# Program order set from a build-time account of engine times, with the delta rule's preparation, its scan and the convolutions as separate parts

## The chip, the cores and the metric

The kernel runs on one core of a Trainium2 chip. The metric is the device time of one execution in microseconds (us). The core's engines are named as in the profile: PE is the matmul engine (TensorE), DVE is VectorE, ACT is ScalarE, POOL is GpSimd, SP is SyncE, which here only issues DMA transfers. Each engine executes its own queue of instructions in the order in which the program placed them, and waits at an instruction until its operands are there.

## What is computed

One layer of a hybrid model on 640 tokens: 128 context tokens and 512 latent tokens, 2048 columns wide. The tokens are normalised and modulated, projected by `w_in`, and then go through two kinds of mixing: four Fourier groups (a two-dimensional FFT, real part) and twelve heads of a bidirectional gated delta rule. The results, each multiplied by its SiLU gate, go through one output projection, a gated residual and a final norm.

```python
h = rms_norm(x) * (1 + scale) + shift
u_f, z_f, qkv, z_d, ab = split(h @ w_in)
y_f = fourier_mix(u_f) * silu(z_f)
q, k, v = silu(short_conv(qkv))            # three taps along the tokens
q, k = l2norm(q) / sqrt(128), l2norm(k)
# per head and direction, S is 128 x 128; g, beta from ab
S_t = g_t (I - beta_t k_t k_t^T) S_{t-1} + beta_t k_t v_t^T
o_t = S_t^T q_t
# in chunks: A = I + strict_lower(beta k k^T decay);  T = A^-1
# u = T (beta v); w = T (beta k e^g); v_new = u - w S; S = S e^gl + kd^T v_new
y_d = rms_norm(o_forward + o_backward) * silu(z_d)
out = final_norm(x + gate * (concat(y_f, y_d) @ w_out)),  state_new = S at the end of the context
```

## The kernel before, in words

The 640 tokens are five tiles of 128; tile 0 is the context. Up to about 185 us the kernel computes the norm, the modulation and the columns of the first head. Then `stream()` (L1003) runs over 50 tiles of 128 columns of `w_in`. For each tile it issues 96 matmuls of 128x320 at L1015: 16 row blocks, three passes of a high and low part each, two halves of the tokens. The weights are loaded by ACT's DMA queue and split by ACT (L136) and POOL (L137). From head 2 on a head is four such tiles, k, v, q and the gate z of the head before, 384 stream matmuls. Behind the stream `out_stream()` multiplies 16 blocks of y by `w_out`, 15 matmuls of 128x512 to a block in its first pass (L1208). The blocks come in the order heads 0 to 10, Fourier groups 0 to 3, head 11.

Beside the stream run Python generators, which issue the small work between the stream's matmuls:

- **Convolution**: `conv` (L538) works on the finished tile of k, v or q at once, on ACT and DVE (L548 to L554).
- **Solve** of head h, `solve(h)` (L596): the inverse of the chunk's triangular matrix. PE's matmuls pk (L624), then DVE's masks, a trip through memory that lays the blocks out as NP (L643, L646), on DVE small steps of growing size (L658 multiply, L660 sum), and then ten product pairs (`prod`: L670 multiply, L672 sum), 512 or 1024 wide on 40 partitions. It ends in DD (L689 to L695), loaded from memory again.
- **Delta** of head h, `delta(h)` (L701), one generator for both of these. *Preparation*: v to tokens (L563), the gate matrices E and the products with q and k (L722 to L728), then a chain of PE groups with copies between them: px (L740), YT (L753), ET (L768, which needs TA from DVE, L756 and L757), EU (L775), the norm of q as jq (L786) and q (L790, a small DVE instruction on PE's result). *Scan*: five steps, in each of which both directions advance one tile. PE: pks and pqs (L805, L812) from the state S; DVE: r (L808); PE: pv (L823); ACT: vn (L826); PE: pu and po (L831, L844); DVE: S (L839). The first step needs neither S nor r; the last has no pu.
- **Head out** (L870), **Fourier** group f (L899; matmuls L928, L935, L940), **residual gates** (L959).

The order is set by hand-written numbers. Each `yield lat, busy` of a generator says how long its step takes and how much of PE's time it adds. A clock advances by 0.82 with each piece of six stream matmuls and by 3.25 with each 15 matmuls of the output projection. A generator is resumed once the clock has passed its due time. The stream itself waits in one place: a k or q tile of head h may be consumed only when `delta(h-2)` is issued, a v tile when v of head h-1 has been read (`needs`, L1086). A scheduler of the framework then orders among instructions that are ready; what it makes of both programs is what the rows of the built order below show.

## Time and profile before

| what | before |
|---|---|
| time of three runs | 1528.46, 1534.41, 1538.11 us (median 1534.41) |
| the profiled execution: time, span | 1528.22 us, 1526.2 us |
| PE busy | 1407.7 us, 92% |
| weight loads on PE (beside the matmuls) | 1270.9 us, 83% |
| DVE busy | 882.6 us, 58% |
| ACT busy, POOL busy | 635.1 us, 643.5 us, 42% each |

The span is the time between the first and the last record of the profiled execution; about 2 us lie around it. A busy share is an average over the whole span. An engine's idle time counts only where the end of the kernel waits for it, so the views below go by stretches and by waits.

### The profile page before, as it was taken

How to read it: one execution, taken by the hardware profiler on the slowest of the kernel's cores; microseconds unless marked ns; L12 is line 12 of the kernel's file. 1: busy time of each engine (PE TensorE's matmuls, PEld its weight loads, DVE VectorE, ACT ScalarE, POOL GpSimd, SP SyncE). 2: the span in 40 equal slices, each digit the busy share in tenths (PEclk: the TensorE clock that was granted, in tenths of full speed). 3: DMA queues.
4: the chain of work that ended last, by engine and by line, in shares of the span. 5: the costliest groups of instructions: out<-in, count | busy, mean ns of one | idle time of the engine just before them, and what ended most of it. 6: DMA issues, size and time to landing. Idle time of an engine off the chain costs nothing. (4 is left out here: it accounts for less than half of the span.)

```text
span 1526.2 us, 27377 instructions
## 1 busy us (share of the span) xinstructions
PE 1407.7 (92%) x10548; PEld 1270.9 (83%) x10548; DVE 882.6 (58%) x1594; ACT 635.1 (42%) x1678; POOL 643.5 (42%) x759
## 2 busy tenths in 40 slices
PE   6999989889989998989999898999999999999996
PEld 5676989788878897978999898888988998888885
DVE  4455257586867677394756748394856534422025
ACT  5343375244262543526254353526353244322234
POOL 2223346425252542434364344444363433236575
PEclk9999999899999999999999999999999999999999
DMA  9899434315253544433223223323233336386103
GB/s 309 294 336 318 149 114 124 86 39 148 89 157 104 153 119 121 136 96 84 76 84 82 77 80 89 91 72 85 77 95 96 104 114 193 120 301 193 56 1 138
DMA packets 251664, 198.35 MB, mean 130 GB/s; under 512 B 43465, under 2 KB 221590, under 8 KB 251406
## 3 DMA queue, kind: packets, MB, share of 16 engines
q1 hardware_dynamic: 130926, 124.77, 25.5%
q10 hardware_dynamic: 120608, 71.84, 16.5%
q8 instruction: 83, 1.36, 0.4%
q14 instruction: 47, 0.39, 0.1%
HBM read 172.57 MB, written 23.99 MB: 129 GB/s over the span
## 5 line engine op out<-in xcount | busy, mean ns | idle before, releaser
L137 POOL TENSOR_TENSOR wlo<-raw,whi 128x512 fp32r<-128x512 f32 (+1 forms) x276 | 382.1, 1389 | 583.1 <-ACT whi L136 481.1
L1015 PE MATMUL mbank<-h_hi,whi 128*128 128x320 f32 x1600 | 522.9, 327 | 0.0
L1015 PE MATMUL mbank<-h_hi,wlo 128*128 128x320 f32 x1600 | 506.9, 317 | 4.3 <-POOL wlo L137 4.2
L1015 PE MATMUL mbank<-h_lo,whi 128*128 128x320 f32 x1600 | 506.8, 317 | 0.0
L1015 PEld LDWEIGHTS mbank<-h_hi,whi 128*128 128x128 f32 x1600 | 309.8, 194 | 10.5 <-issue 7.9
L1015 PEld LDWEIGHTS mbank<-h_hi,wlo 128*128 128x128 f32 x1600 | 308.6, 193 | 7.3 <-POOL wlo L137 5.6
L1015 PEld LDWEIGHTS mbank<-h_lo,whi 128*128 128x128 f32 x1600 | 309.8, 194 | 1.9 <-issue 1.6
L136 ACT CAST whi<-raw 128x512 fp32r<-128x512 f32 (+1 forms) x276 | 168.2, 614 | 241.1 <-PE mbank L1015 60.8
L670 DVE TENSOR_TENSOR tmp<-NP,XB 40x1024 f32<-40x1024 f32 (+1 forms) x60 | 109.9, 1832 | 1.3
L670 DVE TENSOR_TENSOR tmp<-XB,YB 40x1024 f32<-40x1024 f32 (+1 forms) x60 | 105.8, 1763 | 1.0
L818 POOL TENSOR_SCALAR kd<-k,edl 128x128 f32<-128x128 f32 x96 | 59.8, 634 | 41.6 <-PE bank L831 41.4
L548 ACT COPY pj<-mbank 128x128 f32<-128x128 f32 (+2 forms) x99 | 30.0, 339 | 87.5 <-PE mbank L1015 68.1
L1208 PE MATMUL mbank<-wlo,y_hi 128*128 128x512 f32 x160 | 62.8, 393 | 2.8 <-POOL wlo L137 2.0
L805 PE MATMUL bank<-S,KT 128*128 128x128 f32 x192 | 36.5, 301 | 30.4 <-DVE S L839 30.4
L1208 PE MATMUL mbank<-whi,y_hi 128*128 128x512 f32 x160 | 63.8, 399 | 0.0
L726 ACT ACTIVATE E<-gb,ngg 128x128 f32<-128x128 f32 x120 | 42.2, 394 | 51.8 <-DVE AT L728 31.6
L1208 PE MATMUL mbank<-whi,y_lo 128*128 128x512 f32 x160 | 62.4, 390 | 0.0
L1208 PE MATMUL bank<-whi,y_lo 128*128 128x512 f32 x160 | 62.3, 389 | 0.0
L1208 PE MATMUL bank<-whi,y_hi 128*128 128x512 f32 x160 | 62.3, 389 | 0.0
L1208 PE MATMUL bank<-wlo,y_hi 128*128 128x512 f32 x160 | 62.2, 389 | 0.0
L672 DVE TENSOR_REDUCE YB<-tmp 40x64 f32<-40x512 f32 (+2 forms) x60 | 59.7, 995 | 1.4
L672 DVE TENSOR_REDUCE XB<-tmp 40x64 f32<-40x512 f32 (+2 forms) x60 | 59.7, 995 | 1.3
(319 smaller groups left out, 2440.8 us busy)
## 6 DMA issues: line engine op xcount, KB each, us to landing
raw<-in_w_in ACTq DMA_DIRECT2D x104, 512.0 KB
wm<-in_w_mod SPq DMA_DIRECT2D x64, 512.0 KB
gw<-in_w_mod SPq DMA_DIRECT2D x32, 512.0 KB
raw<-in_w_out ACTq DMA_DIRECT2D x48, 256.0 KB
gb<-gd SPq DMA_DIRECT2D x12, 640.0 KB
yd<-zs SPq DMA_DIRECT2D x16, 320.0 KB
zl<-yd SPq DMA_DIRECT2D x16, 320.0 KB
yd<-zl SPq DMA_DIRECT2D x16, 320.0 KB
```

Of the source, the lines that this page charges most:

```text
L136: ACT.copy(whi, raw_part)
L137: sub.tensor_tensor(wlo, raw_part, whi, ALU.subtract)
L548: ACT.copy(pj[:, a:b], ps)
L670: DVE.tensor_tensor(tv, A.unsqueeze(2).broadcast_to(s4), B.rearrange("p j c -> p c j").unsqueeze(1).broadcast_to(s4), ALU.mult)
L672: DVE.tensor_reduce(dst, tv, AX.X, ALU.add)
L726: ACT.activation(E[:, 1 - d], gb[:, d, P * t:P * (t + 1)], AF.Exp, bias=ngg4[:, d, h, t:t + 1])
L805: PE.matmul(pks[:, P * d:P * (d + 1)], lhsT=KT[:, a:a + P], rhs=S[:, d], start=True, stop=True)
L818: POOL.tensor_scalar(kd[:, d], k[:, tt[d], :], edl4[:, d, h, tt[d]:tt[d] + 1], 1.0, ALU.mult, ALU.mult)
L1015: PE.matmul(pm[:, 0:320], lhsT=w, rhs=h[k][:, a:b], start=n == 0, stop=n == 3 * NK - 1)
L1208: PE.matmul(acc[t], lhsT=a[kk][:, sl], rhs=w, start=kk == order[0] and j == 0, stop=kk == order[-1] and j == 2)
```

## The change

It replaces the hand-written numbers by an account. A class `Estimate` is called at every instruction that the program issues. It keeps, for each engine, when it would be free, and for each tile when it would be written and read; the cost of an instruction comes from a small formula per engine. A generator's step now yields nothing. It is resumed when the estimated end of what it issued last, plus 0.2, has been reached by PE's estimated time, or it says "poll" and is asked again.

Further: `delta` becomes two generators, `prep` (up to q) and `scan`, so that the preparation of the next head may stand ahead of the scan of this one. The convolutions and the gate tiles become generators in steps; a k, v, q, z or f tile counts as done at the end of these, not at their start. The Fourier groups also wait for the delta of head 10. The load of DD waits until the head before has used DD. The tiles v and th get two buffers instead of one. Every engine is issued the same instructions as before.

```diff
+class Estimate:
+    MATMUL, WIDE = 13.5, 1 / 2.4
...
+    def __call__(self, inst, *_):
...
+        t = self.free[engine]
+        for x in ins:
+            y = self.of(x.tensor)
+            t = max(t, y[0] + (0.1 if y[1] != engine else 0.0))
...
+            end = t + self.cost(op, engine, inst, outs, ins)
+            self.free[engine] = end
...
+    est = Estimate()
+    nc.push_inst_callback(est)
...
-    def conv(col, parts, dst):
+    def conv(kind, h, parts):
...
         ACT.mul(dst, pj[:, 0:641], cw[:, ct:ct + 1])
+        yield
         DVE.scalar_tensor_tensor(dst, pj[:, 1:642], cw[:, 36 + ct:37 + ct], dst, ALU.mult, ALU.add)
         DVE.scalar_tensor_tensor(dst, pj[:, 2:643], cw[:, 72 + ct:73 + ct], dst, ALU.mult, ALU.add)
+        yield
+        th = g.tile([P, 641], F32, tag="th", name="th", bufs=2)
         ACT.activation(th, dst, AF.Tanh)
+        yield
         DVE.scalar_tensor_tensor(dst, th, 1.0, dst, ALU.add, ALU.mult)
+        yield
+        done.add((kind, h))
...
         for c0 in (0, 8):
             prod(X2[:, 24:32, c0:c0 + 8], X2[:, 24:32, 16:32], YB[:, :, c0:c0 + 8])
-            yield 3.00, 0
+            yield
         xd = dram.tile([40, 32, 32], F32, tag="xd", name="xd", bufs=2)
         SP.dma_start(out=xd, in_=X2)
+        while h and ("dd", h - 1) not in done:
+            yield "poll"
...
-    def delta(h):
+    def prep(h):
         s = st_h[h]
-        KT, QT, k = s["KT"], s["QT"], s["k"]
-        s["v"] = v = g.tile([P, 5, P], F32, tag="v", name="v", bufs=1)
+        KT, QT = s["KT"], s["QT"]
+        s["v"] = v = g.tile([P, 5, P], F32, tag="v", name="v", bufs=2)
...
         s["q2"] = q2 = g.tile([P, 5], F32, tag="q2", name="q2", bufs=3)
         DVE.tensor_scalar(q2, pq[:, 0:320].rearrange("p (t c) -> p t c", c=64)[:, :, 0], HD * EPS, HD * EPS * EPS, ALU.mult, ALU.add)
+
+
+    def scan(h):
+        s = st_h[h]
+        KT, QT, k, v, T, AT = [s[x] for x in ("KT", "QT", "k", "v", "KK", "AT")]
         while h and ("out", h - 1) not in done:
-            yield 5.50, 0
+            yield "poll"
...
+    def advance():
+        moved = True
+        while moved:
+            moved = False
+            for x in list(live):
+                while x in live and (x[2] is None or x[2] + GUARD <= est.free["PE"]):
+                    poll = x[2] is None
+                    resume(x)
+                    if poll and x[2] is None:
+                        break
+                    moved = True
...
-            while not {("u", f), ("f", f), "E_last"} <= done:
-                yield 8.00, 0
+            while not {("u", f), ("f", f), "E_last", ("delta", NH - 2)} <= done:
+                yield "poll"
...
-    live = [[x(), 0.0] for x in (outs, deltas, solves, fouriers, res_gates)]
-    clock, running = 0.0, True
+    for i, kind in enumerate("kvq"):
+        begin(1, conv(kind, 0, i + 1))
+    for rank, steps in enumerate((outs, scans, preps, solves, fouriers, res_gates)):
+        begin(2 * rank, steps())
+    running = True
```

What this does to the order is counted in the built programs, in stream matmuls of 128x320 on PE:

| head | 3 | 4 | 5 | 6 | 7 | 8 | 9 |
|---|---|---|---|---|---|---|---|
| product pairs on DVE between the first and the last r of the scan, before | 7 | 9 | 8 | 8 | 8 | 8 | 8 |
| the same, after | 2 | 2 | 7 | 3 | 3 | 7 | 3 |
| from the first pv of the scan to its last po, before | 202 | 206 | 200 | 200 | 200 | 200 | 200 |
| the same, after | 55 | 51 | 123 | 85 | 65 | 118 | 81 |
| from pk of the next head to this scan's first pv, before | 132 | 114 | 138 | 138 | 138 | 138 | 138 |
| the same, after | 257 | 270 | 163 | 241 | 259 | 164 | 239 |
| from YT to ET in the preparation, before | 24 | 24 | 24 | 24 | 24 | 24 | 24 |
| the same, after | 54 | 60 | 36 | 24 | 60 | 36 | 24 |

On DVE, before, at the start of a scan in the middle of the stream (XB, YB, NP and tmp are solve's, r and S the scan's, QT the convolution's):

```order
L778 COPY KK<-bank 64x5x64
L790 TENSOR_SCALAR q_8994<-bank 128x5
L551 SCALAR_TENSOR_TENSOR QT<-pj,cw,QT 128x641
L658 TENSOR_TENSOR tmp<-NP,XB 40x4
L552 SCALAR_TENSOR_TENSOR QT<-pj,cw,QT 128x641
L660 TENSOR_REDUCE XB<-tmp 40x4
...
L660 TENSOR_REDUCE XB<-tmp 40x4x7
L670 TENSOR_TENSOR tmp<-NP,XB 40x512
L672 TENSOR_REDUCE YB<-tmp 40x8x8
L587 SCALAR_TENSOR_TENSOR zs<-zs,mbank 128x320
L670 TENSOR_TENSOR tmp<-XB,YB 40x512
L808 SCALAR_TENSOR_TENSOR r<-bank,neg_eg,v 128x128 x2
```

The instruction q stands ahead of solve's first small step (L658), and one whole product pair, the first half of the second and a gate tile (L587) ahead of the first r. After the change the scan of head 4 begins like this on DVE; product pairs are L789 and L791, q is L911, r L934, S L965:

```order
L911 TENSOR_SCALAR q_7368<-bank 128x5
L789 TENSOR_TENSOR tmp<-XB,YB 40x1024
L791 TENSOR_REDUCE XB<-tmp 40x8x16
L984 TENSOR_TENSOR o<-o,bank 128x128
L934 SCALAR_TENSOR_TENSOR r<-bank,neg_eg,v 128x128 x2
L789 TENSOR_TENSOR tmp<-XB,YB 40x1024
L791 TENSOR_REDUCE XB<-tmp 40x8x8
L965 SCALAR_TENSOR_TENSOR S<-S,egl,bank 128x128 x2
L980 TENSOR_TENSOR o<-o,bank 128x128 x2
L934 SCALAR_TENSOR_TENSOR r<-bank,neg_eg,v 128x128 x2
L789 TENSOR_TENSOR tmp<-XB,YB 40x1024
L791 TENSOR_REDUCE XB<-tmp 40x8x8
```

Eight pairs stand ahead of the first r, one behind it and one behind the second; q stands among the pairs.

On PE, before, three of a scan's groups (S and r of L805 and L823 as above, vn and kd of L831; the lines left out are stream matmuls of L1015, 24 between two groups):

```order
L805 MATMUL bank<-S,KT 128x128 x2
L812 MATMUL bank<-S,QT 128x128 x2
L1015 MATMUL mbank<-h_hi,whi 128x320
...
L1015 MATMUL mbank<-h_hi,wlo 128x320
L823 MATMUL bank<-r,KK 128x128 x2
L1015 MATMUL mbank<-h_hi,whi 128x320
...
L1015 MATMUL mbank<-h_hi,wlo 128x320
L831 MATMUL bank<-vn,kd 128x128 x2
L844 MATMUL bank<-vn,AT 128x128 x2
```

After the change a scan step of head 4 on PE (pks L931, pqs L938, pv L949, pu L957, po L970, stream L1142):

```order
L931 MATMUL bank<-S,KT 128x128 x2
L938 MATMUL bank<-S,QT 128x128 x2
L1142 MATMUL mbank<-h_lo,whi 128x320
L949 MATMUL bank<-r,KK 128x128
L1142 MATMUL mbank<-h_hi,wlo 128x320
L949 MATMUL bank<-r,KK 128x128
L1142 MATMUL mbank<-h_hi,whi 128x320
L1142 MATMUL mbank<-h_lo,whi 128x320
L1142 MATMUL mbank<-h_hi,wlo 128x320
L1142 MATMUL mbank<-h_hi,whi 128x320
L957 MATMUL bank<-vn,kd 128x128 x2
L970 MATMUL bank<-vn,AT 128x128 x2
```

The groups of a step stand one to four stream matmuls apart, where 24 stood.

On PE behind the stream, before (L928, L935 and L940 are Fourier group 0, L823, L831, L844 and L805 the scan of head 11; the lines left out are matmuls of the output projection, 15 and one):

```order
L823 MATMUL bank<-r,KK 128x128 x2
L928 MATMUL bank<-dft,V 128x256
...
L831 MATMUL bank<-vn,kd 128x128 x2
L844 MATMUL bank<-vn,AT 128x128 x2
L935 MATMUL bank<-dft,A 128x128 x2
L940 MATMUL bank<-fbd,A 128x128 x8
L805 MATMUL bank<-S,KT 128x128 x2
L812 MATMUL bank<-S,QT 128x128 x2
...
L823 MATMUL bank<-r,KK 128x128 x2
```

After the change, all of it at the 120th to 122nd matmul of the output projection (L861, L874, L890, L897 and L907 are px, YT, ET, EU and jq of head 11; L1055, L1062, L1067 a Fourier group; L949 the first pv of head 11's scan):

```order
L861 MATMUL bank<-DD,KK 32x32 x20
L1055 MATMUL bank<-dft,uT 128x256
L1055 MATMUL bank<-dft,V 128x256
L874 MATMUL bank<-DD,YT 32x32 x20
L1055 MATMUL bank<-dft,V 128x256 x2
L890 MATMUL bank<-TA,KK 64x64 x10
...
L897 MATMUL bank<-KK,ET 64x64 x10
L1062 MATMUL bank<-dft,A 128x128 x2
L1067 MATMUL bank<-fbd,A 128x128 x8
L907 MATMUL bank<-cst,jq 128x64 x5
L949 MATMUL bank<-v,KK 128x128 x2
```

The preparation and the scan of head 11 were issued before and into the output projection's first 139 matmuls; now they and the Fourier groups begin at the 120th.

## Rows read from the trace of the kernel before

**Rows 1.** The page: busy us, share of the span and instructions of each engine.
```profile
PE 1407.7 (92%) x10548; PEld 1270.9 (83%) x10548; DVE 882.6 (58%) x1594; ACT 635.1 (42%) x1678; POOL 643.5 (42%) x759
```

**Rows 2.** Windows: stretch, length, then PE, PEld, DVE, ACT, POOL busy us (instructions), PEclk, DMA.
```profile
185.00:520.00 335.00, 298.63 (x2353) 271.97 (x2352) 235.08 (x397) 147.87 (x415) 146.09 (x193) 0.97 0.39 111
520.00:1265.00 745.00, 695.70 (x5697) 666.00 (x5694) 476.34 (x857) 321.76 (x909) 325.07 (x401) 0.97 0.33 96
1265.00:1526.00 261.00, 247.27 (x1174) 206.14 (x1172) 84.30 (x165) 88.75 (x178) 125.03 (x103) 0.99 0.42 143
```

**Rows 3.** Windows, the same columns: about one head in the middle.
```profile
842.00:928.00 86.00, 79.20 (x637) 76.77 (x637) 57.07 (x102) 38.07 (x109) 38.22 (x49) 0.96 0.29 82
```

**Rows 4.** Waits of PE from 520 to 1265 us: total us, times, longest us.
```profile
PE bank L805 <- DVE S L839: 27.8, 14, 4.5
PE bank L768 <- DVE TA L756: 6.2, 6, 1.0
PE bank L768 <- DVE TA L757: 5.9, 6, 1.0
PE bank L823 <- DVE r L808: 3.3, 2, 1.7
PE bank L831 <- ACT vn L826: 3.0, 5, 0.6
```

**Rows 5.** Timeline of DVE: start us, length us, instruction [idle before it <- releaser].
```profile
818.38 0.16 DVE L790 TENSOR_SCALAR q<-bank 128x5 f32<-128x5 f32 x1 [6.05 <-PE bank L786]
...
819.87 0.15 DVE L658 TENSOR_TENSOR tmp<-NP,XB 40x4 f32<-40x4 f32 x1
...
825.58 1.10 DVE L670 TENSOR_TENSOR tmp<-NP,XB 40x512 f32<-40x512 f32 x1
...
838.29 2.38 DVE L670 TENSOR_TENSOR tmp<-NP,XB 40x1024 f32<-40x1024 f32 x1
840.70 1.21 DVE L672 TENSOR_REDUCE YB<-tmp 40x64 f32<-40x1024 f32 x1
...
842.23 0.59 DVE L839 SCALAR_TENSOR_TENSOR S<-S,egl,bank 128x128 f32<-128x128 f32 x2
```

**Rows 6.** Timeline of SP's queue: the load of solve's first operand.
```profile
803.17 1.60 SPq L646 DMA_DIRECT2D NP<-pd  x4
```

**Rows 7.** Timeline of PE: a scan step and the stream behind it.
```profile
842.62 0.86 PE L805 MATMUL bank<-S,KT 128*128 128x128 f32 x4 [3.07 <-DVE S L839]
...
844.66 0.47 PE L1015 MATMUL mbank<-h_hi,wlo 128*128 128x320 f32 x1
844.93 0.47 PE L1015 MATMUL mbank<-h_hi,whi 128*128 128x320 f32 x1
...
847.12 0.31 PE L1015 MATMUL mbank<-h_lo,whi 128*128 128x320 f32 x1
847.26 0.31 PE L1015 MATMUL mbank<-h_hi,wlo 128*128 128x320 f32 x1
```

**Rows 8.** Waits of DVE from 520 to 1265 us, the longest.
```profile
DVE q L790 <- PE bank L786: 48.8, 9, 6.0
```

**Rows 9.** Timeline of PE: two scan steps that stand close together.
```profile
771.12 0.75 PE L805 MATMUL bank<-S,KT 128*128 128x128 f32 x4 [0.43 <-DVE S L839]
...
775.53 0.49 PE L805 MATMUL bank<-S,KT 128*128 128x128 f32 x2
```

**Rows 10.** Timeline of PE: the preparation's ET, its first part.
```profile
803.75 0.33 PE L768 MATMUL bank<-TA,KK 64*64 64x64 f32 x2 [1.03 <-DVE TA L756]
```

**Rows 11.** Timeline of PE: two matmuls of the output projection.
```profile
1285.20 0.39 PE L1208 MATMUL bank<-whi,y_hi 128*128 128x512 f32 x1
1285.42 0.39 PE L1208 MATMUL bank<-wlo,y_hi 128*128 128x512 f32 x1
```

**Rows 12.** Lines of PE from 1265 us: one group of the Fourier matmuls, all four parts.
```profile
L940 PE MATMUL bank<-fbd,A 128*128 128x128 f32 x64 | 8.0, 279 | 0.3 <-ACT A L929 0.3
```

**Rows 13.** Timeline of PE: the first matmuls (pk) of a head's solve.
```profile
787.75 1.28 PE L624 MATMUL bank<-KT 128*128 128x128 f32 x10
```

More of the change, by code (lines that the diff above doesn't have):

```diff
@@ L500, in gates @@
         ACT.activation(edl, edl, AF.Exp)
[L501 to L502 removed]
+        yield
+        gT = g.tile([24, NT], F32, tag="o", name="gT", bufs=1)
         pb, pb2 = bank(), bank()
@@ L587, in after_z @@
             DVE.scalar_tensor_tensor(zs[:, a:b], zs[:, a:b], 1.0, p, ALU.add, ALU.mult)
+        yield
         SP.dma_start(out=yd[k], in_=zs)
+        yield
+        done.add(("z", k - 4) if k > 3 else ("f", k))
     def load_z(k):
@@ L761, in delta @@
                 ACT.copy(T[o, 1 - d, :, cc], pv[i])
-        yield 3.00, 1.1
+        done.add(("dd", h))
+        yield
         lo, up = slice(0, 64), slice(64, 128)
```

295 lines of the change are left out of this document (195 added, 100 removed).

## The prediction, made before the changed kernel ran

> **What bounds the kernel now.** I read the page first. TensorE (PE) is busy 92% of the span, VectorE (DVE) 58% [rows 1]; the span is 1526.2 us. So PE sets the end, and the question is where its other 8% lie. The windows answer that: from 520 to 1265 us, the stretch of heads 2 to 11, PE is busy 695.70 of 745 us (49.3 idle) at a mean granted clock of 0.97; from 185 to 520 it lacks 36 us, after 1265 about 14 [rows 2]. One head in the middle takes about 86 us of PE, with 79.20 busy, and 57.07 busy on DVE [rows 3]: DVE is not full, yet PE waits for it. The list of waits names the places [rows 4]: the first group of a scan step (pks, L805) for the state S, 27.8 us; L823 for r, 3.3; L831 for vn, 3.0; and in the preparation ET (L768) for TA, 6.2 and 5.9.
>
> Why S is late is read on DVE [rows 5]. DVE stood 6.05 us at the one small instruction q (L790), which waits for PE's norm matmuls. Behind q in its queue stood the small steps of the next head's triangular solve (L658), whose operand had long been loaded [rows 6], and behind those the ten wide product pairs (L670 and L672). So the pairs slid into the scan: a pair that begins at 838.29 ends at 841.91, and S starts only after it, at 842.23. PE got S 3.07 us late [rows 7]. In this stretch DVE lost 48.8 us at q, in nine heads [rows 8].
>
> The clock is the second loss. After the 3.07 us wait the stream matmuls follow each other at 0.27 us (844.66, 844.93) and a few us later at 0.14 to 0.15 (847.12, 847.26) [rows 7]: the granted clock went from the lower level, 1.2 GHz, back to 2.4. A mean of 0.97 over 745 us is 745 x 0.03 x 2 = 45 us at the lower level. A matmul there takes 0.12 us longer of 0.27, so these 45 us cost about 20.
>
> **The change part by part.** Each engine gets the instructions that it had; only places in the queues and three buffer counts move. So every term is a wait.
>
> *Scan of heads 2 to 9.* 34.1 us now (27.8 + 3.3 + 3.0) [rows 4]. In the built order DVE has the product pairs mostly ahead of the scan: of heads 3 to 9, 56 pairs stood between the first and last r before, 27 now (two or three a head, seven in heads 5 and 8). Against that, PE's scan steps move together: about 12 stream matmuls apart instead of 24, so 12 x 0.147 = 1.8 us of cover a step less. What a step needs is seen where two stand close without a pair between: 771.12 to 775.53, 4.4 us, with 0.43 of wait at its start [rows 9]. A pair is 3.6 us [rows 5], S behind it 0.6: 4.2; PE's cover from vn to the next S is the pv group and four matmuls, then pu, po and about seven: 0.6 + 0.6 + 0.9 + 1.0 = 3.1, worked out with 0.15 us a matmul. So a pair that falls in a step leaves 0.6 (where r and S share its shadow) to 1.1 us. 27 pairs give 16 to 30; I take 22. Term: 22 - 34 = **-12**. Bounds: -34 (no wait left) and +2 (all stay, and 27 x 1.1 with vn's on top).
>
> *Preparation.* ET's two waits cost 12.1 us [rows 4]; one of a pair is 1.03 us [rows 10]. Before, ET stands 24 stream matmuls (3.5 us) behind YT, and lacks some 2.0 us. Now it stands 36 to 60 behind (5.3 to 8.8 us) in six of heads 3 to 10, and 24 in two. Two heads keep 2.0: 4 left, term **-8** (bounds -12 and 0).
>
> *Clock.* The lower level follows these waits of 1 to 3 us. If waits of that size stay in about four of ten heads, 8 of the 20 us stay: **-12** (bounds -20 and 0).
>
> *185 to 520 us.* The order hardly differs, the waits there are on loads of weights and on the first heads: 0 (bounds -10 and +10, a quarter of the 36 us idle either way).
>
> *After the stream.* Head 11 and the four Fourier groups stood one step to 15 matmuls of the output projection; now head 11's preparation and scan, and fouriers 0 and 1, stand packed from the 120th to the 159th. The spacing there is 0.22 us [rows 11], so 39 matmuls cover 8.6 us. The chain: four preparation steps of at most 3.5 + 0.5 us (the 24 matmuls plus a quarter of the 2.0), 16 in all, and four and a half scan steps of 4.4, 20: together 36 us. PE's own work inside it: 67 small and 42 large matmuls, about 10 us at 0.15 for the large and 0.05 for the small; the Fourier groups, 2.0 each in L940 alone [rows 12], at least 4. 36 - 8.6 - 10 - 4 = 13; with the other Fourier matmuls, which I put at twice that of L940, 8. Term **+10** (bounds 0, since the waits now are small there, and +28, only the output matmuls as cover).
>
> *Split of the convolutions, second buffers of v and th.* Their work is ACT's and DVE's, neither full [rows 1], and only k, v and q are read later: 0. If the cover is gone, a convolution of one tile is late by its own length, and that is in rival A.
>
> Sum against the profiled execution's 1528.2 us: -12 - 8 - 12 + 0 + 10 = -22, **1506 us**. The three runs reach from 1528.5 to 1538.1, and the profiled one lies 6 us below their median of 1534.4; I add a third of that and say 1508. That is 1.7% below the median; about 1%, 15 us, is what a measurement of this kernel can tell from no change.
>
> **The rivals.**
>
> *A, slower: the pairs come too late for the packed scan.* DVE must now finish its pairs before the first r, and the whole scan of a head waits on that one point. From the head's first solve matmuls at 787.75 [rows 13] the operand is loaded at 803.17 + 1.6 = 804.8 [rows 6]: 17 us. The small steps take 819.87 to 825.58, 5.7; five pairs 825.58 to 838.29, 12.7, and each further one 3.6 [rows 5]. So eight pairs are done 17 + 5.7 + 23.5 = 46.2 us after, three after 30.3. In the new order PE has, between the same matmuls and the first pv, 270 stream and 67 other matmuls for head 4: 270 x 0.147 + 67 x 0.15 = 49.7 us; for head 5, 163 and 66: 33.9. (0.15 for the others is (79.2 - 384 x 0.147 - 2.5) / 134.) The slack is 3 to 4 us, and DVE does convolutions meanwhile. It decides from about 4 us late; at 6 us late beyond that in seven heads, 42 us, with the clock's gain of 12 lost: 1506 + 54 = 1560. For it: so little slack. Against: DVE has 29 us free per head [rows 3] and no longer stands at q. 0.13.
>
> *B, no change: the waits only move.* The pairs are as long as before, 3.6 us, and every step that meets one waits 3.1 as now. Then 34 stay, the clock's 20 stay, the preparation gives 8, the tail takes 10: 1530. For it: 27 pairs are still in the scans, and closer steps give less cover. Against: 771.12 [rows 9]. The Trainium skill, on the page Perfetto Trace Analysis, section "Optimizing Scalar/DVE Operations", says that where Scalar or Vector are not saturated but cause bubbles on others, breaking up instructions may let work end sooner; this change leaves each as long as it was, and by that rule alone it would come out as B. The trace agrees that DVE is unsaturated and that one 2.38 us product holds S back; it also shows 6.05 us at q, which no splitting would mend. 0.24.
>
> *C, more gain:* the packed scans run without any wait, the clock stays up, and the tail hides: -34 - 12 - 20 = -66, 1462. For it, the step at 771.12. Against, seven pairs each in heads 5 and 8. 0.10.
>
> *That nothing changes* in the order is excluded by the rows of the built order.
>
> **How the numbers follow.** The forecast has 0.53, its own range 1488 to 1524. A, B and C have 0.13, 0.24 and 0.10. To leave out no more than 2 in 10, the range takes in B with its spread up to 1542 and stops at 1478, short of C and of A's worse half. Faster by over 1% (below 1519): nearly all of the forecast, 0.50, and C, 0.10: 0.60. Within 1%: 0.26, B and the upper edge of the forecast. Slower: 0.14, A and a little of B.
>
> **What would show it.** In the profile after: the wait of PE's pks for S from 520 to 1265 at 15 to 25 us; DVE's wait at q near zero; ET's waits at about 4; the clock there at 0.98 to 0.99; after the stream some 10 us more idle, at YT, ET and pks. I am wrong if PE waits at the first pv or pks of a head for several us (A), if the wait at S stays at 28 and the clock at 0.97 (B), or if a load, a buffer of k or v or the weight split on GpSimd holds the stream, of which I have no term.

## The result: slower by 0.8%

The changed kernel takes 1543.88 us (median of 15 runs, 1533.99 to 1555.05), the kernel before 1530.66 us (15 runs beside it). The ratio is 1.0076, 95% interval 1.0052 to 1.0099. The forecast was 1508.

The profiled execution takes 1539.05 us, against 1528.22: 10.8 more. The page of the changed kernel, in the form of [rows 1] (with the span):

```profile
span 1537.3 us, 27379 instructions
...
PE 1412.6 (92%) x10548; PEld 1272.0 (83%) x10548; DVE 904.7 (59%) x1594; ACT 630.9 (41%) x1678; POOL 650.0 (42%) x759
```

PE is busy 4.9 us more, the span is 11.1 longer, so PE idles 6 us more. To see where, both traces are cut at the same points of PE's work: the 1152nd stream matmul (of 128x320), the 4416th, and the 240th matmul of the output projection. Between the first two lie most of heads 3 to 11; between the last two lie the end of the stream and the tail.

| stretch | before | after | difference |
|---|---|---|---|
| start to the 1152nd stream matmul | 459.6 | 454.1 | -5.5 |
| to the 4416th (heads 3 to 11) | 737.8 | 729.9 | -7.9 |
| to the 240th of the output projection (tail) | 151.6 | 176.0 | +24.4 |

The windows of the last two stretches, of the kernel before (columns as in [rows 2]):

```profile
459.60:1197.40 737.80, 682.57 (x5511) 648.09 (x5510) 502.71 (x875) 315.99 (x899) 319.91 (x402) 0.97 0.33 95
1197.40:1349.00 151.60, 150.86 (x1024) 137.63 (x1024) 59.19 (x172) 57.22 (x131) 51.88 (x50) 1.00 0.45 143
```

and of the changed kernel:

```profile
454.10:1184.00 729.90, 675.13 (x5546) 637.95 (x5546) 511.39 (x860) 314.74 (x902) 324.05 (x408) 0.97 0.33 94
1184.00:1360.00 176.00, 164.85 (x1087) 148.98 (x1086) 80.53 (x193) 61.38 (x146) 56.99 (x55) 0.96 0.39 121
```

In heads 3 to 11 PE idled 737.80 - 682.57 = 55.2 us before and 729.90 - 675.13 = 54.8 after. So no idle time was gained there. The 7.4 us of busy time that this stretch lost have two sources. The clock, 0.97 in both to two digits, is 0.968 before and 0.974 after as the mean of forty equal windows: some 9 us less at the lower level, which by the spacings of [rows 7] (0.12 of each 0.27) is about 4. And the small work is cut differently: of PE's instructions the start has 97 fewer (3200 for 3297), heads 3 to 11 have 35 more and the tail 63 more.

In the tail the idle time goes from 0.7 to 11.2 us, +10.4. The clock goes from 1.00 to 0.96: 176 x 0.04 x 2 = 14 us at the lower level, which cost some 6. The other 8 of the 24.4 are the moved work. In the start PE is busy 410.26 us before and 408.55 after, so it idles 3.8 less. The ledger is then -3.8, -0.4 and +10.4 us of idle time, and 4.9 more busy time over the whole span, which is about what the clock of the whole span costs (0.975 before, 0.972 after: 10 us more at the lower level, some 4 to 5). Together that is +11.1, the difference of the spans.

The stretch from 520 to 1265 us of the changed kernel, to be read beside [rows 2]:

```profile
520.00:1265.00 745.00, 688.72 (x5526) 657.90 (x5526) 507.08 (x855) 320.61 (x916) 332.86 (x408) 0.98 0.33 93
```

This window ends in the tail, so it holds other work than the same window before. PE's waits are therefore read in heads 3 to 11 as cut above. Before, the rows that differ from [rows 4] are:

```profile
PE bank L805 <- DVE S L839: 28.6, 15, 4.5
PE bank L823 <- DVE r L808: 8.4, 5, 2.8
```

After (L931 pks, L949 pv, L957 pu, L890 ET, L897 EU, L1003 head out's transposes, L1108 and L1098 residual gates):

```profile
PE bank L949 <- DVE r L934: 18.3, 13, 5.2
PE bank L1003 <- DVE o L993: 13.8, 7, 3.8
PE bank L897 <- ACT ET L892: 5.7, 2, 3.4
PE bank L1098 <- DMA gw<-in_w_mod: 4.1, 4, 2.3
PE bank L957 <- ACT vn L952: 4.0, 3, 2.1
PE bank L931 <- DVE S L965: 2.8, 7, 0.6
PE bank L890 <- DVE TA L877: 2.0, 1, 2.0
```

The waits of the scan (S, r, vn) went from 28.6 + 8.4 + 3.0 = 40.0 to 2.8 + 18.3 + 4.0 = 25.1; S nearly vanished, r took its place. Those of the preparation, ET 12.1 and YT 2.9, went to 2.0. That is 28 us less. But groups that hardly waited before now do: head out's o 13.8, EU 5.7, the gates 5.6 (4.1, and 1.5 for ga), and two more 1.8, together 26.9, where 0.2 stood. In the window of [rows 4], 520 to 1265 us, S, r and vn are 2.8, 16.7 and 6.3, and zs, in the tail, adds 3.7. DVE no longer stands at q, which was 48.8 us in [rows 8]:

```profile
DVE q L911 <- PE bank L907: 1.4, 2, 1.0
```

Its longest wait in that window is now at zs for ACT, 57.6 us in 18. So the one thing that the prediction most wanted gone is gone, and PE waits as long as before.

What the new waits are is read from four places of the changed kernel. The first is head out, on all engines (columns as in [rows 5]):

```profile
703.24 0.31 ACT L990 ACTIVATE jk<-o 128x128 f32<-128x128 f32 x1 [0.35 <-DVE o L980]
...
706.18 0.31 ACT L990 ACTIVATE jk<-o 128x128 f32<-128x128 f32 x1
...
707.20 1.27 POOL L255 TENSOR_TENSOR wlo<-raw,whi 128x512 fp32r<-128x512 f32 x1
708.44 1.18 POOL L992 TENSOR_TENSOR m<-m,cst 128x5 f32<-128x5 f32 x1
...
709.65 1.88 DVE L993 TENSOR_TENSOR o<-o,m 128x640 f32<-128x640 f32 x1 [2.87 <-POOL m L992]
...
711.59 0.66 PE L1003 MATMUL bank<-cst,o 128*128 128x128 f32 x4 [3.77 <-DVE o L993]
```

Here the norm of a head's output is a chain over four engines: five squares jk on ACT, between which convolution steps now stand; a power on POOL, behind the weight split of L255; the product o on DVE; and PE's transposes. In the stream these stand 26 to 38 stream matmuls behind the last po, where 46 to 50 stood before, and here PE waits 3.77 us. The distance is not all of it: the two longest of these waits, 3.77 and 3.58 us, stand at 35 and 38. The chain itself is long here; the product o alone takes 1.88 us, and its median over the twelve heads is 0.83. The second is ACT:

```profile
679.11 0.38 ACTq L1126 DMA_DIRECT2D raw<-in_w_in  x1
679.52 0.43 ACT L673 COPY pj<-mbank 128x320 f32<-128x320 f32 x1 [3.36 <-POOL wlo L255]
679.85 0.63 ACT L952 ACTIVATE vn<-bank,s 128x128 f32<-128x128 f32 x2
```

ACT stood 3.36 us at the issue of a weight load (raw, L1126), which waits until POOL has split (wlo, L255) the block that held its buffer. Behind it in ACT's queue stood the convolution's copy and vn, for which pu waits; elsewhere (at 847 and 1101 us, 3.99 and 3.33 us) ET's copy stood there, for which EU waits. The third is DVE at the start of a scan:

```profile
682.15 2.02 DVE L789 TENSOR_TENSOR tmp<-XB,YB 40x1024 f32<-40x1024 f32 x1
684.20 1.21 DVE L791 TENSOR_REDUCE XB<-tmp 40x128 f32<-40x1024 f32 x1
...
685.53 0.59 DVE L934 SCALAR_TENSOR_TENSOR r<-bank,neg_eg,v 128x128 f32<-128x128 f32 x2
```

A whole product pair, 2.02 + 1.21 us, ends and only then r runs: one pair ahead of r where [rows 5] had one ahead of S. PE waited 2.10 us for it. The fourth is PE in the tail:

```profile
1264.24 0.79 PE L1363 MATMUL mbank<-whi,y_hi 128*128 128x512 f32 x1 [3.69 <-DVE zs L703]
```

The output projection waits 3.69 us for a bank that DVE's gate step zs of head 11 has yet to read.

### The profile page after: what moved, and what is told of

Read it like the earlier page. It is cut to its first block, busy times and chain, and to the rows that moved or that the text cites. A ratio compares the mean times of both kernels' runs of the same rounds, so it can differ in the third digit from the quotient of the medians.

```text
span 1537.3 us, 27379 instructions
## 1 busy us (share of the span) xinstructions
PE 1412.6 (92%) x10548; PEld 1272.0 (83%) x10548; DVE 904.7 (59%) x1594; ACT 630.9 (41%) x1678; POOL 650.0 (42%) x759
## 3 DMA queue, kind: packets, MB, share of 16 engines
q8 instruction: 83, 1.36, 0.4%
## 5 line engine op out<-in xcount | busy, mean ns | idle before, releaser
L255 POOL TENSOR_TENSOR wlo<-raw,whi 128x512 fp32r<-128x512 f32 (+1 forms) x276 | 385.6, 1403 | 527.0 <-ACT whi L254 429.8
L1142 PE MATMUL mbank<-h_hi,whi 128*128 128x320 f32 x1600 | 512.8, 321 | 0.0
L1142 PE MATMUL mbank<-h_hi,wlo 128*128 128x320 f32 x1600 | 507.6, 317 | 0.0
L1142 PE MATMUL mbank<-h_lo,whi 128*128 128x320 f32 x1600 | 507.2, 317 | 0.0
L1142 PEld LDWEIGHTS mbank<-h_hi,whi 128*128 128x128 f32 x1600 | 307.1, 192 | 5.4 <-issue 3.8
L1142 PEld LDWEIGHTS mbank<-h_lo,whi 128*128 128x128 f32 x1600 | 307.1, 192 | 3.6 <-issue 3.3
L1142 PEld LDWEIGHTS mbank<-h_hi,wlo 128*128 128x128 f32 x1600 | 306.7, 192 | 1.6 <-issue 1.2
L944 POOL TENSOR_SCALAR kd<-k,edl 128x128 f32<-128x128 f32 x96 | 52.9, 562 | 143.3 <-PE bank L957 143.2
L789 DVE TENSOR_TENSOR tmp<-NP,XB 40x1024 f32<-40x1024 f32 (+1 forms) x60 | 106.1, 1768 | 1.3
L789 DVE TENSOR_TENSOR tmp<-XB,YB 40x1024 f32<-40x1024 f32 (+1 forms) x60 | 100.7, 1679 | 0.9
L952 ACT ACTIVATE vn<-bank,s 128x128 f32<-128x128 f32 x120 | 37.5, 365 | 66.4 <-PE bank L949 61.9
L791 DVE TENSOR_REDUCE YB<-tmp 40x64 f32<-40x512 f32 (+2 forms) x60 | 59.8, 997 | 1.2
L791 DVE TENSOR_REDUCE XB<-tmp 40x64 f32<-40x512 f32 (+2 forms) x60 | 59.8, 996 | 1.2
L949 PE MATMUL bank<-r,KK 128*128 128x128 f32 x192 | 39.0, 303 | 21.9 <-DVE r L934 21.7
```

Source lines behind the costliest of these rows:

```text
L255: sub.tensor_tensor(wlo, raw_part, whi, ALU.subtract)
L789: DVE.tensor_tensor(tv, A.unsqueeze(2).broadcast_to(s4), B.rearrange("p j c -> p c j").unsqueeze(1).broadcast_to(s4), ALU.mult)
L791: DVE.tensor_reduce(dst, tv, AX.X, ALU.add)
L944: POOL.tensor_scalar(kd[:, d], k[:, tt[d], :], edl4[:, d, h, tt[d]:tt[d] + 1], 1.0, ALU.mult, ALU.mult)
L949: PE.matmul(pv[:, P * d:P * (d + 1)], lhsT=T[:, 1 - d, tt[d], :], rhs=r[:, d] if step >= 0 else v[:, 0, :], start=True, stop=True)
L952: ACT.mul(vn[:, d], pv[:, P * d:P * (d + 1)], s["s3"][:, d, tt[d]:tt[d] + 1])
```

## The experiments

All ratios are against the kernel before, with 95% intervals. In each expectation two theories (in e7 three) stand against each other; the text after each says which the run bore out. The second buffer of th, the wait of DD and the later Fourier groups were not run by themselves. Line numbers in rows of edited kernels are shifted by the edit's few lines.

**Which part of the change costs?** The first question is why the account packs the scan. A head of four tiles takes 139 us in the account, of which PE's own work is 75 (trace: 86, 729.9 us for 34 tiles). In the account the stream stands still at tile ends, and small steps are issued there close together. The account charges waits to loads of weights (tile raw); that most of the standing comes from them is a reading of the account, which no trace shows.

*e1: the account ignores the wait for a loaded weight.*

```diff
             y = self.of(x.tensor)
+            if x.tensor.name.startswith("raw"):
+                continue
```

> The changed kernel, but its account no longer lets ACT stand still at a weight block that is still being loaded (tiles raw); nothing else is edited, and the instructions are the same. In the changed kernel's account a head takes 139 us, of which PE's own work is 75, while the trace shows 86 us a head; the stream then stands still in the account at the ends of tiles, and several small steps are issued there with no stream matmul between them. Theory 1 (the account is too slow, and the clumped steps are what waits): steps are spread over the head again, PE's wait at head_out for o falls from 16 us to under 5, r's wait from 22 to under 12, the stretch of heads 3 to 11 gets 10 to 20 us shorter, and the kernel takes 1515 to 1530 us. Theory 2 (DVE's product pairs are too much for any packed or half packed scan): the waits move, and it stays within 6 us of the changed kernel, 1538 to 1550.

Measured: 1542.17 us, 1.0091 [1.0058, 1.0123]. PE's waits do not fall: in heads 3 to 11 r has 42.3 us in ten waits (18.3 in the changed kernel), and PE idles 66.4 us in that stretch. The waits at EU and vn are gone or small there and o has 10.3, but TA has 10.4. PE, one pv:

```profile
768.39 1.01 PE L951 MATMUL bank<-r,KK 128*128 128x128 f32 x3 [5.39 <-DVE r L936]
```

This pv stands six stream matmuls behind its pks (761.07 us), and between the two DVE runs two product pairs ahead of r. Theory 2.

*e2: preparation and scan again one generator.*

```diff
             yield from prep(h)
-            done.add(("prep", h))
...
-            while ("prep", h) not in done:
-                yield "poll"
             yield from scan(h)
```

> The changed kernel with prep and scan of a head issued by one generator again, as delta was; the account stays. Theory 1 (the account alone makes the order; in it the preparation of the next head never overtakes the scan of this one, because the next q tile waits for the delta two heads back and the solve is late): the same waits at r and o, within 5 us of the changed kernel, 1538 to 1550. Theory 2 (the split is what moved the scans together and made them wait): it goes back towards the kernel before, 1525 to 1535, with r's wait under 12 us.

Measured: 1532.86 us, 1.0030 [1.0012, 1.0048], 11 us less than the changed kernel by the medians, 7 by the ratios. The waits of heads 3 to 11 remain (r 17.2 us, o 14.5, EU 6.8), as theory 1 had it, but the time is the one that theory 2 named. Of the profiled executions (1534.46 and 1539.05 us) the tail takes 9 us less and heads 3 to 11 take 2 less, the start 7 more. So the split costs some 7 to 11 us inside this change, and not by the waits of the scan; by what, is not shown.

*e3: head out is held back 7 us of the account.*

```diff
         zs = load_z(4 + h)
         yield
+        due = est.free["PE"] + 7.0
+        while est.free["PE"] < due:
+            yield "poll"
```

> The changed kernel, with head_out held back by 7 us of the account's PE time after its gate tile is loaded, so that PE meets its transposes later. Theory 1 (the wait for o at head_out, 16 us in nine heads, is a loss of its own that a later place takes away): that wait falls under 4 us, nothing else grows by more than 5, and the kernel takes 1528 to 1536 us. Theory 2 (whatever is held back only lets the next head's chain, which needs the same o buffer, wait instead): the waits at pv, pu and pks of the next scan grow by the same 12 us, and it stays at 1540 to 1550.

Measured: 1543.97 us, 1.0099 [1.0070, 1.0127]. The waits of PE in heads 3 to 11:

```profile
PE bank L938 <- DVE q L911: 15.5, 5, 3.6
...
PE bank L1006 <- DVE o L993: 8.9, 7, 2.1
```

o fell to 8.9 us and r to 10.2; but pqs, behind q, now waits 15.5, vn 11.8 and TA 8.2, and PE idles 67.3 us in the stretch. The wait that was removed came back at others. Theory 2.

*e7: the kernel before, hand-written numbers, with only the split (and two buffers of v).*

```diff
+    def scan(h):
...
             yield from delta(h)
+            done.add(("prep", h))
+
+    def scans():
+        for h in range(NH):
+            while ("prep", h) not in done:
+                yield 0.50, 0
+            yield from scan(h)
             done.add(("delta", h))
```

> The kernel before, with delta split into preparation and scan as separate generators and two buffers for v, and the hand-written numbers kept. Theory 1 (the split alone neither gives nor takes much; the account makes the order): 1524 to 1536 us, PE's wait for S over 20 us. Theory 2 (the split lets the next head's preparation push q and the products later on DVE): 1540 or more. Theory 3 (it starts preparation earlier and so frees DVE earlier): under 1520.

Measured: 1551.92 us, 1.0141 [1.0117, 1.0166]. In heads 3 to 11 pks waits 39.7 us for S, and the matmuls of the norm of q wait 12.3 for jq. The split, with its buffer of v, costs 21 us: theory 2's time, and S waits 39.7 where it waited 28.6.

*e6: the changed kernel with convolutions and gates issued at once.*

```diff
-                begin(1, conv(kind, i, halves(res)))
+                for _ in conv(kind, i, halves(res)):
+                    pass
```

> The changed kernel with the third part undone: the convolutions and the gate tiles are issued at once when their tile of the stream is finished, as before, not in steps. In the changed kernel ACT stood 3.3 to 4.3 us at the issue of a weight load that waited for POOL's split, and behind it stood ET's copy, vn and a convolution's copy; PE then waited at EU (5.7 us), pu (6.3) and head_out. Theory 1 (the convolutions in steps are what put these behind the load): EU and pu waits fall under 3 us in all, head_out's under 8, and the kernel takes 1530 to 1537 us. Theory 2 (the load stands in ACT's queue in every version, and what is hit is chance): the sum of PE's waits in heads 3 to 11 stays at 50 to 60 us, 1538 to 1550.

Measured: 1562.32 us, 1.0213 [1.0187, 1.0240]; r 27.1 us, o 17.3, TA 13.8, YT 9.2. Theory 1 is right on EU and pu, whose waits are gone in heads 3 to 11. It is wrong on o, which did not fall, so the convolution's steps between the squares are not what makes that wait; and it is wrong on the time, since r, TA and YT wait more. Convolutions in steps are worth some 18 us here, which no term of mine held. With e2 and e7 the parts come out as: the split alone +21; account and steps without the split +3; account and split without the steps +32; all of them +13. They do not add up.

**Does another distance help?**

*e5: e1, and 18 more stream matmuls between pks and pv.*

```diff
                     PE.matmul(pqs[:, P * d:P * (d + 1)], lhsT=QT[:, a:a + P], rhs=S[:, d], start=True, stop=True)
-                yield
+                yield from pause()
```

> The kernel of e1_load (account without the wait for a weight block's load), in which PE stood 5.4 to 6.4 us once in each of seven heads at pv, 6 stream matmuls behind its pks, because r stood behind two product pairs on DVE. One more edit: after pks a scan step lets three pieces of the stream (18 more matmuls, 2.6 us) pass before pv, unless the stream stands still. Theory 1 (what PE waits is DVE's delay less the distance that the order leaves between pks and pv): that wait falls by 2.6 us a head, from 42 to 20 to 26 us in all, and the kernel takes 1515 to 1528 us. Theory 2 (the later pv only lets the rest of the scan run into the end of the tile, and the wait returns at pks or at head_out): 1536 to 1545.

Measured: 1549.49 us, 1.0125 [1.0107, 1.0144]. Two steps of a scan on PE:

```profile
848.55 0.61 PE L941 MATMUL bank<-S,KT 128*128 128x128 f32 x4
...
855.65 1.22 PE L959 MATMUL bank<-r,KK 128*128 128x128 f32 x4 [2.54 <-DVE r L944]
...
865.93 1.22 PE L941 MATMUL bank<-S,KT 128*128 128x128 f32 x4 [4.50 <-DVE S L975]
```

pv's wait falls to 2.54 us here, but the next pks waits 4.50 for S. In heads 3 to 11 r has 23.8 us, which is theory 1's fall, and S, 0.5 in e1, has 16.5. In time, and in the wait that returns, it is theory 2: DVE has the same pairs to do, and PE meets them one group later.

*e9: the account ignores the wait for raw from the k tile of head 10 on.*

```diff
+            if self.skip and x.tensor.name.startswith("raw"):
+                continue
...
+            est.skip = est.skip or (kind, i) == ("k", 10)
```

> The changed kernel; only from the k tile of head 10 on does its account, as in e1_load, no longer let ACT stand at a weight block that is being loaded. Up to head 8 the order is the same; head 11's preparation then stands in the last stream tile and not at the 120th matmul of the output projection, and fourier 0 behind it. Theory 1 (the end of the kernel lost some 15 us because the account ran late there): from the stream's 4416th matmul to the 240th of the output projection PE needs 10 to 18 us less than in the changed kernel (176 us), and the kernel takes 1527 to 1535 us. Theory 2 (what was moved out of the stream is work that PE has to do in any case): as much longer before, and 1540 to 1548.

Measured: 1541.57 us, 1.0064 [1.0045, 1.0082]. The window of the tail:

```profile
1199.80:1357.40 157.60, 153.20 (x1036) 138.54 (x1036) 65.32 (x176) 57.67 (x136) 52.82 (x51) 1.00 0.44 135
```

The tail falls from 176.0 to 157.6 us, idle 4.4 for 11.2, clock 1.00, as theory 1 had it: the order packed behind the stream costs idle time and clock there. But 51 of PE's instructions moved out of this window (1036 for 1087), and the stretch before it took them in and idles more (59.6 us for 54.8): the 4416th stream matmul ends at 1199.8 us, not 1184.0, and the two traces part only behind the 3840th (0.7 us apart there, 13.4 at the 4032nd). Over the whole next to nothing is gained. The time is theory 2's.

**Was the stand at q the cause?**

*e4: the kernel before, with jq, its matmuls and q issued ahead of px.*

```diff
+        jq = g.tile([P, 641], F32, tag="th", name="jq", bufs=1)
+        ACT.activation(jq, QT, AF.Square)
+        yield 1.00, 0
...
+        DVE.tensor_scalar(q2, pq[:, 0:320].rearrange("p (t c) -> p t c", c=64)[:, :, 0], HD * EPS, HD * EPS * EPS, ALU.mult, ALU.add)
         if h == NH - 1:
             done.add("E_last")
...
-        jq = g.tile([P, 641], F32, tag="th", name="jq", bufs=1)
...
```

> The kernel before with one block moved: the norm of q (jq on ACT, its five matmuls, q on DVE) stands ahead of px instead of behind EU. It tests the reading that S came late in the kernel before because DVE stood at q, with solve's small steps and product pairs queued behind it. Theory 1 (that reading is right): DVE's wait at q falls from 49 us to under 10, more product pairs end ahead of the scan, PE's wait for S falls from 30 us to under 12, and the kernel takes 1505 to 1520 us. Theory 2 (the pairs fall into the scan anyway, since they start when their operand is loaded and last 30 us): q's wait goes to the next instruction that needs PE (KK behind EU), PE's wait for S stays over 20, and it stays at 1525 to 1535.

Measured: 1501.42 us, 0.9813 [0.9782, 0.9843]. This is faster than both kernels, by 28 us and by 42. PE's waits and DVE's longest one:

```profile
PE bank L805 <- DVE S L839: 29.8, 20, 3.1
PE bank L823 <- DVE r L808: 13.1, 8, 3.9
```

```profile
DVE KK L788 <- PE bank L785: 39.9, 8, 6.5
```

and the window of heads 3 to 11:

```profile
457.40:1172.50 715.10, 669.99 (x5510) 638.68 (x5510) 522.57 (x875) 314.95 (x901) 339.56 (x402) 0.98 0.34 98
```

The time lies below what either theory gave. The wait for S did not fall, 29.8 us where this stretch had 28.6, only into smaller pieces (20, where 15 stood), and r waits more, as theory 2 had it. DVE next stands at KK (L788), behind the same matmuls of EU; its stands at q and KK together were 46.3 + 29.7 = 76.0 us before in this stretch. So my reading of S in [rows 5] is not borne out: with nearly half of that standing gone, S waits as long.

What fell is ET's, YT's and vn's waits, from 18.0 us to 0.2, so that PE idles 45.1 us instead of 55.2. Why ET's fell is seen on DVE. Before, the two copies of TA, for which the two parts of ET wait, each stand behind a convolution step of v (L551 and L552):

```profile
801.99 1.34 DVE L551 SCALAR_TENSOR_TENSOR vT<-pj,cw,vT 128x641 f32<-128x641 f32 x1 [1.02 <-ACT vT L550]
803.36 0.34 DVE L756 STREAM_TRANSPOSE TA<-bank 32x160 f32<-32x160 f32 x1
803.73 0.89 DVE L552 SCALAR_TENSOR_TENSOR vT<-pj,cw,vT 128x641 f32<-128x641 f32 x1
804.65 0.35 DVE L757 STREAM_TRANSPOSE TA<-bank 32x160 f32<-32x160 f32 x1
```

In e4 the preparation is a step later, and both stand behind the last of v's steps:

```profile
710.82 0.83 DVE L554 SCALAR_TENSOR_TENSOR vT<-th,vT 128x641 f32<-128x641 f32 x1 [0.81 <-ACT th L553]
711.68 0.34 DVE L766 STREAM_TRANSPOSE TA<-bank 32x160 f32<-32x160 f32 x1
712.05 0.35 DVE L767 STREAM_TRANSPOSE TA<-bank 32x160 f32<-32x160 f32 x1
```

This gain has nothing to do with the stand at q, which comes behind ET. Of the 23 us of this stretch, 10 are idle time and, by the clock (1526.2 x 0.025 x 2 = 76 us at the lower level before, 1502.7 x 0.020 x 2 = 60 here, of the whole span), some 7 are clock; the rest stays open.

*e8: e4, and the copy of EU's result that DVE made goes to ACT.*

```diff
-        for d, (ra, rb, cp) in enumerate(((lo, up, DVE.tensor_copy), (up, lo, ACT.copy))):
+        for d, (ra, rb, cp) in enumerate(((lo, up, ACT.copy), (up, lo, ACT.copy))):
```

> The kernel of e4_before_q (q's norm ahead of px), in which DVE next stood 39.9 us in eight heads at KK, the copy of EU's lower half, with solve's steps behind it. Here that copy is ACT's too, as the upper half's. Theory 1 (each instruction on which DVE stands for PE delays the product pairs behind it): KK's wait is gone, pairs start about 5 us earlier a head, PE's waits for S and r fall from 43 to under 25 us, 1485 to 1497 us. Theory 2 (ACT, which stands at its own weight loads, makes the copy late and the scan's first pv waits): 1500 or more.

Measured: 1507.86 us, 0.9853 [0.9830, 0.9876]. The stand at KK is gone, DVE next stands at QT behind ACT (51.6 us), and PE waits 38 us for S and r (31.0 and 7.2). Taking one place away where DVE stands moved it to another, and S waits no less. The time is theory 2's.

*e10: the same move of q in the changed kernel.* The edit is that of e4, in `prep`.

> The changed kernel with the norm of q ahead of px, the edit that made the kernel before 28 us faster (e4_before_q). Theory 1 (that edit gained because DVE no longer stood at q; in the changed kernel DVE stands at q for less than 1 us in all, so there is nothing to gain): 1538 to 1550. Theory 2 (it gains in any order, by taking one link out of the chain behind EU): 1515 to 1530.

Measured: 1526.14 us, 0.9964 [0.9942, 0.9985]: 18 less than the changed kernel, theory 2's time. The link that theory 2 names is not shown as its cause. Yet DVE stood at q for 1.4 us only in that order. Of the profiled executions (1530.08 and 1539.05 us) the start takes 10 us less, the tail 5 less, and heads 3 to 11 take 7 more, with 54.7 us of idle time, as without it. So the gain has nothing to do with the stand at q. The two profiled executions differ by 9 of the 18 us; what brings the rest is open.

**What do the product pairs cost?** The next runs change the pairs themselves.

*e11 and e12: each pair multiplies and sums one element of each row, in the changed kernel (where the account is charged the full length, so that the order stays near) and in the one before.*

```diff
-            DVE.tensor_tensor(tv, A.unsqueeze(2).broadcast_to(s4),
-                              B.rearrange("p j c -> p c j").unsqueeze(1).broadcast_to(s4), ALU.mult)
-            DVE.tensor_reduce(dst, tv, AX.X, ALU.add)
+            DVE.tensor_tensor(tv, A[:, :, 0:1], B[:, 0:1, 0:1].broadcast_to([40, ni, 1]), ALU.mult)
+            DVE.tensor_reduce(dst[:, :, 0:1], tv, AX.X, ALU.add)
```

> The changed kernel with solve's ten product pairs one element wide per row, so that a pair takes about 0.3 us where it took 2 to 3.6; the account is still charged the full width. The inverse is left out by this, so the outputs are not the reference's. Theory 1 (the pairs on DVE are what r and S wait for, and only these): r's wait falls from 22 us to under 5, the others (head_out's o 16, ET, vn, the gates, the tail) stay, and it takes 1515 to 1528 us, while e12 takes 1480 to 1495. Theory 2 (the pairs also keep DVE from o, TA and the convolutions): both come to within 10 us of each other, under 1500.

Measured: 1489.44 us, 0.9734 [0.9695, 0.9774]. PE's waits in heads 3 to 11:

```profile
PE bank L1006 <- DVE o L996: 16.9, 8, 3.1
PE bank L900 <- ACT ET L895: 5.1, 2, 2.8
PE bank L960 <- ACT vn L955: 4.6, 2, 3.8
```

> The kernel before with the product pairs one element wide, as in e11; the inverse is left out. Theory 1: PE's wait for S falls from 30 us to under 5, those for ET and TA stay at 12, the lower clock falls from 44 to under 15 us between heads 3 and 11, and it takes 1480 to 1495 us, 30 us or so less than e11: freed of the pairs, the hand-written order is the better one. Theory 2: as e11, within 10 us.

Measured: 1443.23 us, 0.9424 [0.9389, 0.9458]. The same view of this kernel:

```profile
PE bank L766 <- DVE TA L754: 6.2, 6, 1.0
PE bank L766 <- DVE TA L755: 5.9, 6, 1.0
```

In both, the waits for S and r are gone, and PE idles 30.4 us (e11) and 16.5 us (e12) in heads 3 to 11. That is theory 1 of both expectations on the places; both times came out lower than it had them, by 26 and by 37 us. The pairs cost 1530.7 - 1443.2 = 87 us before and 1543.9 - 1489.4 = 54 after. These costs include what the pairs cost in clock (0.975 for the whole span before, 0.990 in e12). So the new order does shelter PE from the pairs, by 33 us. Freed of the pairs, the hand order is 46 us faster. What is left after is, in heads 3 to 11, the waits that the change made, o 16.9, EU 5.1, vn 4.6; what is left before is ET's 12.1, which the pairs do not touch. Of the profiled executions, 44 us apart, heads 3 to 11 make 22, the tail 17 and the start 5. The balance is 33 gained at the pairs, 46 lost elsewhere, 13 slower.

*e13, e14, e15: each pair of 1024 elements as two of 512, in the kernel before, in the changed one, and in e4.*

```diff
             ni, nj, ncol = A.shape[1], A.shape[2], B.shape[2]
+            if ni * ncol * nj > 512:
+                prod(dst[:, 0:ni // 2], A[:, 0:ni // 2], B)
+                prod(dst[:, ni // 2:ni], A[:, ni // 2:ni], B)
+                return
```

> The kernel before with each product pair of 1024 elements a row (six of ten a head) issued as two of 512, the same elements in all; 144 instructions more on DVE. Theory 1 (a pair's length is what r and S wait out): a scan instruction waits at most 1.9 us for a half where it waited 3.6 for a pair; PE's wait for S and r between heads 3 and 11 falls from 37 us to under 25, and it takes 1505 to 1520 us. Theory 2 (the sum of DVE's work ahead of the scan counts): twelve instructions more a head cost DVE 1 to 2 us a head, PE's wait stays, and it takes 1528 to 1540.

Measured: 1545.40 us, 1.0082 [1.0051, 1.0113]. The cost of a whole pair on DVE before and of a half in e13, both from 520 to 1170 us (lines of the trace; us in all, then ns of one), and PE's waits in heads 3 to 11:

```profile
L670 DVE TENSOR_TENSOR tmp<-XB,YB 40x1024 f32<-40x1024 f32 x21 | 41.2, 1962 | 0.5
L672 DVE TENSOR_REDUCE XB<-tmp 40x64 f32<-40x1024 f32 x14 | 16.9, 1210 | 0.4
```

```profile
L674 DVE TENSOR_TENSOR tmp<-XB,YB 40x512 f32<-40x512 f32 x56 | 75.9, 1356 | 1.7
L676 DVE TENSOR_REDUCE XB<-tmp 40x64 f32<-40x512 f32 (+1 forms) x56 | 37.9, 677 | 1.7
```

```profile
PE bank L809 <- DVE S L843: 45.1, 18, 3.9
PE bank L827 <- DVE r L812: 15.0, 12, 3.3
```

A half is 1.36 + 0.68 = 2.0 us, two are 4.1; a whole pair is 1.96 + 1.21 = 3.2 in the mean (the 2.38 of [rows 5] was a long one). DVE is busy 929.9 us for 882.6 before. The waits for S and r rise to 60 us, from 37, and the time lies above theory 2's too.

> The changed kernel with the same edit; the account charges the halves as it charged the pairs, so that some steps move. Theory 1: r's wait falls from 18 us between heads 3 and 11 to under 10, and it takes 1525 to 1537 us. Theory 2: 1540 to 1552.

Measured: 1546.21 us, 1.0082 [1.0057, 1.0107], 2 above the changed kernel; r keeps 17.6 us. Theory 2.

> The kernel of e4_before_q (1501 us) with the same edit. There PE still waits 43 us for S and r, in 28 pieces of 0.4 to 3.9 us. Theory 1: under 30 us, and 1485 to 1496. Theory 2: 1500 to 1508.

Measured: 1540.16 us, 1.0040 [1.0021, 1.0059], 39 above e4 (35 by the ratios), far above theory 2's 1500 to 1508. DVE is busy 946.1 us there and 900.8 in e4.

In all three theory 1 is out, and the time goes with the sum of DVE's work: it grew by 47, 12 and 45 us in e13, e14 and e15, and the times by 15, 2 and 39. Because the halves added work, these runs do not show what a shorter instruction would do at an equal sum. The Trainium skill says (Perfetto Trace Analysis, "Optimizing Scalar/DVE Operations") that breaking up instructions may let work be completed sooner where an unsaturated engine causes bubbles on others. These runs do not agree with it for pieces that cost 2.0 us instead of half of 3.2 and stand in the same queue.

## Why the prediction was wrong

**What bounds the kernel: in part.** PE's idle time and the scan's waits were read rightly. The cause that I gave for the wait at S, the stand at q, is not borne out: e4 took the stand away and S still waits 29.8 us. What S and r wait for is DVE's pairs: with these narrowed both waits are gone, and the pairs cost 87 us by e12. That it is their sum more than the length of one is what e13 to e15 point to.

**Scan, -12: it came, at another place.** From 40.0 to 25.1 us in heads 3 to 11, -15; -8 in the window of [rows 4]. I put the rest at S, 15 to 25 us; it stands at r, 18.3, and S has 2.8. Pairs that stood ahead of S stand ahead of r.

**Preparation, -8: it came, but not net.** ET's waits fell by 10.1 us and YT's by 2.9. EU, the next group of the chain, now waits 5.7, since ET's copy on ACT stands behind a weight load's issue.

**The failing step: only waits to be taken away were counted.** "Each engine gets the instructions that it had; only places in the queues and three buffer counts move. So every term is a wait" is right, but between 520 and 1265 us the terms held only the waits that the rows of before show. There was none for places where PE meets other engines anew: head out's o (13.8 us), EU (5.7), the gates (5.6), two more (1.8), and behind heads 3 to 11 zs (3.7). Part of it stood in the order: head out's transposes had moved from 46 to some 30 stream matmuls behind the last po. I counted distances for ET and for the scan's groups and not for these. So 28 us fell, 27 came, and heads 3 to 11 idle 54.8 us against 55.2. The time is near rival B's 1530, to which I gave 0.24, and "the waits only move" is what happened, but not by B's mechanism: B had the waits stay in the scan, where they fell. e3 shows how such a wait moves on: taken from o, it came back at q, vn and TA. Which single place could be freed without another filling up stays open.

**"Their work is ACT's and DVE's, neither full: 0": wrong.** The convolutions in steps were priced at nothing. e6 puts them at 18 us in favour of the change, while ACT's queue with them in it has the waits at EU and vn, which are gone in heads 3 to 11 of e6. A busy share of 42% [rows 1] says nothing on who stands behind whom.

**Clock, -12: about 4 of it came.** The term rests on fewer waits of 1 to 3 us, and in heads 3 to 11 PE waits 42 times where it waited 45. The clock there is 0.974 for 0.968, and 0.98 for 0.97 in the window of [rows 2]. The start, 0.966 for 0.978, gave as much back, and the tail is at 0.96.

**Tail, +10: right in size, wrong in place.** The idle time grew by 10.4 us, but at the 120th matmul of the output projection, where I had the chain of head 11, there is no wait. It is in head 10's scan (vn 2.3, r 1.6), zs (3.7), head out (2.2) and an operand of the output projection (1.3), so the size was luck. The clock's 6 us in the tail had no term. That this order costs idle time there is shown by e9, which gets 6.8 us of it back in the tail and loses 4.8 before it. The term's sum was also loose: with the other Fourier matmuls at twice the 4 us of L940 it leaves 5, not 8.

**From 185 to 520 us, 0:** the nearest stretch that was cut at equal work, from the start to the 1152nd stream matmul, is 5.5 us shorter, 3.8 of it idle time, within the bounds.

Nearly all of the error is the new waits and the clock that did not gain.

Rival A, pairs late for the packed scan, is there: 12.5 of r's 16.7 us between 520 and 1265 stand at the first r of a scan, in six heads, the longest 5.2. That is below the 42 that it supposed.

## What to carry to other kernels

When an order is rebuilt, list for each group of the engine that sets the end how far its operand's last writer stands ahead of it, in both orders, and what else that writer's chain now stands behind; price every group whose distance shrinks or whose chain grows, not only those that wait now. An engine that is 58% busy but holds long work in one queue passes its delay on to whatever stands next: price the sum of that work by taking it away (87 us here) before moving single waits. One small chain moved ahead, q, brought 28 us, where the rebuilt order cost 13; and it did so in part because TA no longer stood behind v's convolution, at which the edit had not been aimed.

## What the runs showed of the hardware that I had not expected

An engine that only issues a transfer can stand in its own queue: ACT stood 3.36 us at a weight load's issue until POOL had split an earlier block, and copies that PE needed stood behind it. Two halves of a product pair take 4.1 us where the whole takes 3.2. And the same DVE instruction need not take the same time: the product o (128x640) takes 0.82 to 0.83 us in all twelve cases of the two kernels' traces in which no POOL instruction runs beside it (nine before, three after), and up to 1.91 before and 1.88 after among those where one does.
